# Finishing a masked sum in two column halves, and adding the first half of its last block to the common sums

## The chip, the cores and the metric

The kernel runs on one NeuronCore of one Trainium2 chip. The metric is the device time of one execution in microseconds (us), as the median of several runs. Times inside an execution are read from the profiled run and count from the start of its instruction span. The span is shorter than the device time: 82.7 of 84.4 us in the kernel before. In the profile lines PE is TensorE, DVE is VectorE and ACT is ScalarE.

## The reference

```python
B, S, D = 8, 8192, 512          # x [B,S,D] f32, lengths [B] int64, w [D,D] f32
masked = x * (pos < lengths)     # pos = 0..S-1
cs = np.cumsum(masked, axis=1)
mid = cs[b_idx, lengths // 2]    # one row of 512 for each batch
return mid @ w                   # [8, 512] f32
```

Only row `lengths // 2` of the running sum is used. So the kernel has to add the first rows of each batch up to there, and multiply the eight sums by `w`. For this draw of lengths that is 31.25 MB to read; the arithmetic is small.

## The kernel before

The rows arrive in blocks of 512: 128 partitions with four rows each (the "row groups" 0 to 3). TensorE adds a block to the sums by a matmul whose weights are 8 columns wide, one column for each batch. Row group j uses column tile j of the array, so its sums stand in the PSUM partitions from 32j on. The four groups run side by side: a block leaves eight records in the profile, two for each group, and all eight fit into 1.04 us (74.98 to 76.03) although one lasts 0.59:

```python
def add(j, weights, rows):                 # rows: 128 x 512
    return pe.matmul(s_ps[32*j:32*j+B], lhsT=weights, rhs=rows, start=False, stop=False,
                     skip_group_check=True, tile_position=(0, 32*j))
def add_column(j, weights, row):           # column quarter j of a row group, in tile j
    return pe.matmul(t_ps[32*j:32*j+B, :P], lhsT=weights, rhs=row[:, P*j:P*(j+1)], ...)
def tell():                                # a one-column matmul that raises TensorE's semaphore
    pe.matmul(idle_ps[:1, :1], lhsT=tick[:], rhs=tick[:], ...).then_inc(s_pe, 1)
```

After the loop over the usual blocks comes the tail. The last block of the last batch (tile `last`) arrives in three pieces: row groups 0 and 1, then 2, then 3. It never goes to the common sums `s_ps`. It goes by column quarters straight to `t_ps`, the layout that the transposes read. `s_ps` gets there by a copy to `s_sb` and a "fold", a matmul that adds the four row groups and spreads the columns over the tiles:

```python
# TensorE, tail
tell()
... add_last(0)        # waits for piece 0: 2 row groups x 4 quarters of 128 columns into t_ps
... fold_half(0)       # waits for s_sb copy 0
... add_last(1)
... fold_half(1)       # waits for s_sb copy 1
... add_last(2).then_inc(s_pe, 1)
... product: wait for transpose 0, 16 matmuls, wait for transpose 1, 16 matmuls    # o_ps = sums @ w

# VectorE (DVE), tail
dve.wait_ge(s_pe, PE_ALL)                  # the tell
for h in range(2): copy s_sb half h <- s_ps half h          # 128 x 256 each
dve.wait_ge(s_pe, PE_SUM)                  # all of t_ps
for h in range(2): transpose t_sb half h <- t_ps
dve.wait_ge(s_pe, PE_OUT); copy o_ps out                     # ScalarE copies the other half
```

## Time and profile before

| What | Before |
|---|---|
| device time, median of 3 runs | 84.37 us (84.34 to 84.56) |
| instruction span of the profiled run | 82.7 us |
| last usual block landed, its adds | 74.52; 74.98 to 76.03 us |
| the three pieces of `last` landed | 75.80, 76.48, 77.10 us |
| tell ended; the two copies ended | 76.01; 77.01 us |
| first transpose started | 77.73 us |
| product | 78.12 to 79.22 us |

The table is read from the bottom up. The product waits for the first transpose, and that starts 0.72 us after the second copy's end. In between lie fold and last adds. Everything above "tell ended" is set by the stream of loads. The lines themselves stand in the prediction.

### The profile page before, as it was taken

What the parts mean: (1) busy time and instruction counts of PE and PEld (TensorE: products, weight loads), DVE (VectorE), ACT (ScalarE), POOL (GpSimd) and SP (SyncE); (2) the same over time, 40 slices, a digit from 0 to 9 for tenths busy, and PEclk for the clock granted to TensorE, in tenths of its full rate; (3) what the DMA queues carried; (4) which work ended last, traced back from release to release, by engine and by line L of the source; (5) the groups of instructions that cost most, each with busy time, mean ns of one, the idle gap of its engine ahead of it and who ended that gap; (6) DMA issues with size and microseconds to landing.
All of it is one profiled execution on the core that took longest, in us unless ns stands there. A gap on an engine that the chain in (4) does not pass through costs nothing. (4 is left out here: it accounts for less than half of the span.)

```text
span 82.7 us, 1481 instructions
## 1 busy us (share of the span) xinstructions
PE 59.9 (72%) x377; PEld 15.8 (19%) x377; DVE 14.9 (18%) x78; ACT 7.4 (9%) x8; POOL 1.3 (2%) x14
## 2 busy tenths in 40 slices
PE   2980799999275199999291099994927999797730
PEld 2400020512020012321020024220201141112510
DVE  2858887001001000001000000000000000001420
ACT  2999100000000000000000000000000000000020
POOL 5000000000000000000000000000000000000000
PEclk9999999999999858999999999999996599999999
DMA  2899999999999999999999999999999999899000
GB/s 32 281 440 428 468 414 402 439 401 436 436 452 398 402 444 408 412 396 432 451 425 404 454 438 411 429 396 468 412 420 452 396 452 436 377 408 356 1 0 8
DMA packets 3538, 31.25 MB, mean 378 GB/s; under 512 B 530, under 2 KB 546, under 8 KB 1202
## 3 DMA queue, kind: packets, MB, share of 16 engines
q1 hardware_dynamic: 2610, 27.27, 78.3%
q10 hardware_dynamic: 928, 3.97, 12.6%
HBM read 31.23 MB, written 0.02 MB: 378 GB/s over the span
## 5 line engine op out<-in xcount | busy, mean ns | idle before, releaser
L505 PE MATMUL s_ps<-xt,cur 128*8 128x512 f32 x184 | 25.2, 669 | 14.3 <-PEq L148 14.3
L518 PE MATMUL idle_ps<-idle 128*128 128x512 f32 x36 | 20.2, 681 | 0.0
L505 PEld LDWEIGHTS s_ps<-xt,cur 128*8 128x8 f32 x184 | 4.2, 93 | 32.7 <-issue 32.7
L469 DVE TENSOR_TENSOR cur<-since 128x16 f32 x9 | 1.7, 188 | 46.6 <-DVEq L148 46.6
L518 PEld LDWEIGHTS idle_ps<-idle 128*128 128x128 f32 x36 | 6.6, 208 | 14.1 <-issue 14.1
L505 PE MATMUL s_ps<-rem,cur_rem 128*8 128x512 f32 x64 | 8.4, 592 | 0.0
L322 ACT COPY o_sb<-o_ps 8x128 f32<-8x128 f32 x2 | 0.5, 258 | 70.8 <-PE o_ps L598 70.8
L505 PE MATMUL s_ps<-first,cur_first 128*8 128x512 f32 x16 | 3.8, 1040 | 2.9 <-DVE since L353 2.9
L266 ACT ACTIVATE rem<-rem 128x2048 uint32<-128x2048 uint32 x3 | 5.5, 1892 | 0.0
L529 PE MATMUL s_ps<-zero 1*128 1x512 f32 x2 | 2.1, 1136 | 1.6 <-DVE zero L353 1.6
L505 PEld LDWEIGHTS s_ps<-rem,cur_rem 128*8 128x8 f32 x64 | 1.9, 93 | 5.7 <-issue 5.7
L353 DVE COPY s_sb<-s_ps 128x256 f32<-128x256 f32 x2 | 0.8, 425 | 9.5 <-PE idle_ps L522 9.5
L511 PE MATMUL t_ps<-last,e_last 128*8 128x128 f32 x32 | 1.7, 273 | 0.0
L478 DVE COPY cur_rem<-table 128x32 f32 x5 | 0.9, 181 | 3.0 <-DVEq L148 3.0
L264 ACT ACT_TABLE_LOAD x1 | 1.3, 1283 | 1.5 <-PEq L619 1.5
L505 PEld LDWEIGHTS s_ps<-first,cur_first 128*8 128x8 f32 x16 | 0.3, 90 | 5.9 <-DMA first<-in_x_dram 4.4
L598 PE MATMUL o_ps<-wt,t_sb 128*8 128x128 f32 x32 | 1.1, 273 | 0.4 <-DVE t_sb L353 0.4
L353 DVE TENSOR_TENSOR part_a<-since,step_a 1x42 f32<-1x42 f32 (+1 forms) x2 | 1.1, 555 | 0.1
L598 PEld LDWEIGHTS o_ps<-wt,t_sb 128*8 128x8 f32 x32 | 0.8, 89 | 0.7 <-issue 0.7
L511 PEld LDWEIGHTS t_ps<-last,e_last 128*8 128x8 f32 x32 | 0.8, 88 | 0.3 <-DMA last<-in_x_dram 0.2
L511 PE MATMUL t_ps<-s_sb,fold 128*8 128x128 f32 x8 | 0.8, 274 | 0.1
L532 PEld LDWEIGHTS n_ps<-len_f,ones 1*128 1x128 f32 x2 | 0.7, 332 | 1.0 <-DVE above L353 0.5
(68 smaller groups left out, 13.7 us busy)
## 6 DMA issues: line engine op xcount, KB each, us to landing
xt<-in_x_dram SPq DMA_DIRECT2D x10, 2048.0 KB, 13.4
xt<-in_x_dram SPq DMA_DIRECT2D x3, 1024.0 KB, 11.0
first<-in_x_dram SPq DMA_DIRECT2D x2, 1024.0 KB, 8.0
rem<-in_x_dram ACTq DMA_DIRECT2D x3, 512.0 KB, 8.1
wt<-in_w_dram ACTq DMA_DIRECT2D x1, 1024.0 KB, 4.9
rem<-in_x_dram ACTq DMA_DIRECT2D x3, 256.0 KB, 7.5
last<-in_x_dram SPq DMA_DIRECT2D x1, 512.0 KB, 6.0
last<-in_x_dram SPq DMA_DIRECT2D x2, 256.0 KB, 6.2
```

The costliest lines, as they stand in the source:

```text
L264: act.memzero(lens1[:, 2 * B:])
L266: act.memzero(rem[:, q]).then_inc(s_rfree[q], 1)
L322: copy = act.copy(out=o_sb[1][:, j * P:(j + 1) * P], in_=o_ps[64 + 32 * j:64 + 32 * j + B, :P])
L353: do(*args, **kw).then_inc(s_dve, 1)
L469: dve.tensor_tensor(out=cur[:, k], in0=since[:, :B, here].rearrange("p b h -> p h b"), in1=since[:, 1:, here].rearrange("p b h -> p h b"), ...
L478: dve.tensor_copy(out=cur_rem[:, k], in_=rests[:, ds(dve.snap(of, min_val=1, max_val=RR - 1), 1), k].rearrange("p o w -> p (o w)"),).then_ ...
L505: return pe.matmul(s_ps[32 * j:32 * j + B], lhsT=weights, rhs=rows, start=False, stop=False, skip_group_check=True, tile_position=(0, 32 * j))
L511: return pe.matmul(t_ps[32 * j:32 * j + B, :P], lhsT=weights, rhs=row[:, P * j:P * (j + 1)], start=False, stop=False, skip_group_check=Tru ...
L518: pe.matmul(idle_ps[:], lhsT=idle[:], rhs=idle[:, :1].to_broadcast((P, D)), start=True, stop=True)
L529: pe.matmul(s_ps[:], lhsT=zero[:], rhs=zero[:, :1].to_broadcast((1, D)), start=True, stop=False, skip_group_check=True)
L532: pe.matmul(n_ps[:, :B], lhsT=ones[:], rhs=len_f[:], start=True, stop=True).then_inc(s_pe, 1)
L598: mm = pe.matmul(o_ps[32 * j:32 * j + B, :P], lhsT=t_sb[:, kc, :B], rhs=wt[:, kc, j * P:(j + 1) * P], start=(kc == 0), stop=(kc == KC - 1) ...
```

## The change

Its intent: take fold and last adds out of those 0.72 us. If each column half has its own PSUM tensor (a "bank"), semaphore and transpose, half 0 can be folded under the second copy, and half 1 under the first transpose. The core of the diff:

```diff
+    ENDS = [(slice(0, 2), slice(0, D)), (slice(2, 3), slice(0, D)),
+            (slice(3, 4), slice(0, D // 2)), (slice(3, 4), slice(D // 2, D))]   # 4 pieces, was 3
-    t_ps = ps("t_ps", [P, D])
+    t_ps = [ps(f"t_ps{h}", [P, D]) for h in range(2)]                           # two tensors
-    nc.scalar.dma_start(out=wt[:], in_=w.rearrange("(p kc) d -> p kc d", kc=KC))
+    for h in range(2):                                  # w in two contiguous halves
+        nc.scalar.dma_start(out=wt[:, 2*h:2*h+2],
+                            in_=w[D//2*h:D//2*(h+1)].rearrange("(p k) d -> p k d", k=2))
   # TensorE, front
-        keep_busy()              # one idle matmul
-            keep_busy(b)         # b = 0, 1: one more
   # TensorE, tail
+        if has_last:
+            pe.wait_ge(s_last[0], 16)
+            for g in range(2):
+                add(g, e_last[:], last[:, g])           # "the join": piece 0 into s_ps
         tell()
-        add_last(0); fold_half(0); add_last(1); fold_half(1); add_last(2)
+        wait piece 1: add_columns(h, e_last, last[:, 2]) for h in 0, 1    # 4 x 64 columns each
+        wait piece 2: add_columns(0, e_last, last[:, 3])
+        wait copy 0:  add_columns(0, fold, s_sb)  -> semaphore for transpose 0
+        wait piece 3: add_columns(1, e_last, last[:, 3])
+        wait copy 1:  add_columns(1, fold, s_sb)  -> semaphore for transpose 1
   # DVE, tail
-        dve.wait_ge(s_pe, PE_SUM)
         for h in range(2):
+            dve.wait_ge(s_pe, PE_SUM + h)
             transpose half h                            # after BOTH copies, as before
```

The tail is shortened to its order here; the code has `If_cmp` and full arguments. Cut: one more memset, semaphore counts.

## The prediction

> **What bounds the kernel now.** I read the page's slices first, then the chain that ended last, then the timeline of the last eight microseconds, then the records of the tile that holds the last rows.
>
> The page, for the span and the transfers (40 slices of 2.07 us each):
>
> ```profile
> span 82.7 us, 1481 instructions
> ...
> DMA  2899999999999999999999999999999999899000
> ...
> DMA packets 3538, 31.25 MB, mean 378 GB/s; under 512 B 530, under 2 KB 546, under 8 KB 1202
> ```
>
> From the third slice to the thirty-seventh the 16 DMA engines are full. The kernel streams 31.25 MB, and everything up to about 76.5 us is this stream. The change moves the same bytes, so only what follows the stream can change: the tail of some 6 us. The chain shows which part of it is work:
>
> ```profile
> 74.61 0.37 issue
> 74.98 1.04 PE s_ps L505 x8
> 76.03 0.08 PE idle_ps L522
> ...
> 76.13 0.44 DVE s_sb L353
> ...
> 76.61 1.09 PE t_ps L511 x24
> ...
> 77.73 0.26 DVE t_sb L353
> 77.99 0.14 issue
> 78.12 1.10 PE o_ps L598 x32
> ...
> 79.24 0.29 DVE o_sb L353
> 79.53 0.02 issue
> 79.56 0.28 DVE o_sb L353
> ```
>
> Read it as: last adds into the common sums, copy to memory, fold onto the transposable layout (t_ps), transpose, product, copy out. But a chain names only one releaser of each step, so I asked for the last rows' tile and the timeline of the fold:
>
> ```profile
> L248 SPq DMA_DIRECT2D last<-in_x_dram x3: 333/333/333, 69.8 to 70.9; - x3
> ...
> DMA to landing us min/median/max: 6.0/6.1/6.2
> ```
>
> ```profile
> 75.85 0.17 PE L522 MATMUL idle_ps<-tick 128*1 128x1 bf16 x1
> 75.85 0.62 PE L511 MATMUL t_ps<-last,e_last 128*8 128x128 f32 x16
> 76.61 0.28 PE L511 MATMUL t_ps<-s_sb,fold 128*8 128x128 f32 x2
> 76.64 0.28 PE L511 MATMUL t_ps<-last,e_last 128*8 128x128 f32 x2
> ```
>
> The three pieces of the last block land at 69.82 + 6.0 = 75.8, about 70.35 + 6.1 = 76.5 and 70.9 + 6.2 = 77.1 us; the trace's landing records say 75.80, 76.48 and 77.10. The second s_sb copy ends at 77.01. So two things meet at 77.1: the third landing, and the second copy. After it come 0.63 us of fold and last adds up to the transpose at 77.73. That 0.63 us is what the change attacks.
>
> [...]an f32 128x512 matmul over four column tiles leaves eight records, and all eight fit into 1.04 us (74.98 to 76.03) although each lasts 0.60; four start together, and their second records start 0.43 us later. [...]The trace's packets: 2 KB took 86 ns, 4 KB 162, 8 KB 324 in the mean. That is about 38 ns for each KB and some 10 ns fixed. 1 KB loads are not in this trace. [...]its clock records show two half-clock stretches of 3.41 us, from 28.4 and 62.5 us[...].
>
> **The change part by part.**
>
> *Front.* Two idle matmul instructions go (3.81 and 10.56 us, 2.08 us each[...]). TensorE waits for loads there: the first block lands at 8.27, the second at 10.76, the first pair of usual blocks at 16.84. Without them the second block's adds (1.9 us) start at 10.8 and end at 12.7; the three idle matmuls of the first round then bridge to about 16.3 and the first pair starts at its landing near 16.9 instead of 17.31. That frees a buffer 0.4 us sooner, with two 2 MB transfers still queued: no effect on a full stream. The weights come as 4 KB packets instead of 8 KB: 256 x 162 against 128 x 324 ns, the same within 0.05 us. One more memset on the DVE near 13.6 us (0.2 us) is used by nobody before 14.5. Sum: 0 to +0.05.
>
> *Last rows.* The first piece (two row groups, 512 KB) is as before, and I expect it at 75.80. Now it is added to s_ps: two instructions, one in column tile 0 and one in tile 1, each 128x512. That is four records, but in each tile two follow each other at 0.43 us, so four records take as long as the eight of a full block: 0.86 us. The tiles are busy with the last usual block until 75.85, so the adds occupy 75.85 to 76.71. Only then can the one-column matmul that tells the DVE run: 76.71 + 0.17 = 76.88 against 76.01 before. This is the part that was free before: sixteen 128-column records in t_ps ran from 75.85 to 76.47, under the first copy.
>
> *Copies.* The DVE starts 0.117 us after the tell (76.013 to 76.13). First copy 76.99 to 77.42, second at the old distance of 0.459: 77.45 to 77.88. They have not shrunk: 128x256 each, 0.425 us.
>
> *Fold and transposes.* Half 0 of the fold starts 0.054 us after the first copy, at 77.47; eight records of 64 columns, done near 77.75, under the second copy. So the fold has gone from the path, as meant. But the DVE's program puts both copies before the first transpose, so that starts at 77.88 + about 0.05 = 77.93. Before: 77.73. Loss: 0.20 us. The fold of half 1 runs 77.93 to about 78.23, the second transpose 78.28 to 78.53.
>
> *Product.* It starts 0.147 us after the first transpose's end: 78.18 + 0.15 = 78.33 against 78.12. The third quarter of it would come 0.44 us later, at 78.77, when the second transpose is done. So 32 records run through, to 79.39 against 79.18.
>
> *Column halves by DMA.* By the fit above a 1 KB packet is 10 + 38 = 48 ns (an estimate from the trace's packets). Eight for each engine make 0.38 us for each half, against 0.61 for the whole piece before. Landings near 76.9 and 77.3; they are needed at 77.47 and 77.93. Both hidden.
>
> Sum: the copies end at 77.88 instead of 77.01 (+0.87), and the first transpose follows them by 0.05 instead of 0.72 us (-0.67): +0.20 us, and 0.02 at the front. 84.37 + 0.22 is about 84.6 us.
>
> **The rivals.** *It gains as intended.* If the sums were not later, say because the first piece lands well before the usual block is done, copies would end at 77.0, the first transpose would start at 77.1, the second at about 77.75 after the last landing, and the product would end near 78.6: 0.55 us won, 83.8 us. For it: 0.63 us of work really leaves the path. Against it: the tiles' free time (75.85) and the landing (75.80) coincide, and 0.86 us must then be streamed whichever was first. *It is hidden, and the last landing stays the bound:* if the 1 KB packets were far slower than the fit, the second half would land after 77.9 and the end would be set by it. Twice the estimate, 96 ns, gives 0.77 us for each half and a last landing at 78.0: 84.8 us or so.[...]
>
> **Range and chances.** The stream is the same, and all differences worked out lie between -0.55 and +0.5 us, under 1% of 84.4. The runs before spread by 0.22. I predict 84.6 us, 84.25 to 84.95 in 8 of 10. Over 2% is 1.7 us[...]: faster 0.01, within 2% 0.98, slower 0.01.
>
> **What would show it.** In the changed profile the chain should run: s_ps adds from the usual block, then s_ps adds from the last rows (about 0.86 us), the tell, both s_sb copies one after the other, the transpose, the product; no t_ps matmul between copies and transpose. The tell should end some 1.05 us after the first piece's landing. The first transpose should start within 0.1 us of the second copy's end. I am wrong if the first transpose starts less than 1.9 us after the first piece lands, if it waits for a landing, or if the stream itself ends at another time than 76.6 +- 0.2 us.

+0.87, -0.67 and +0.02 us at the front on 84.37 make about 84.6.

## More of the kernel before

One line that looks like nothing will matter later. It fixes the instruction slot at which TensorE's program starts, here 80:

```python
pe.addr_align(256, offset=80, max_nops=0)
```

## The result

The changed kernel took 84.59 us (84.54 to 84.73, four runs) against 84.36 (84.34 to 84.56, four runs) of the kernel before in the same rounds. The ratio is 1.0024, with a 95% interval of 1.0004 to 1.0044: the same within 2%, and 0.2 us slower. Here and below a ratio is the mean time of one kernel's fast runs over that of the other's of the same rounds, so it is not quite the ratio of the medians. Executions over 1.5% slower than the fastest of the same kernel are left out of the means.

The page of the changed kernel, the same lines as in the prediction:

```profile
span 82.9 us, 1505 instructions
...
DMA packets 3827, 31.26 MB, mean 377 GB/s; under 512 B 562, under 2 KB 834, under 8 KB 1618
```

The stream moved the same bytes at the same rate. There are 289 packets more, among them the 1 KB ones (the column "under 2 KB"). The chain of waits of the changed kernel (start us, us, what):

```profile
74.96 1.78 PE s_ps L513 x11
...
76.81 0.09 PE idle_ps L532
...
76.92 0.43 DVE s_sb L360
...
77.38 0.43 DVE s_sb L360
...
77.91 0.26 DVE t_sb L360
...
78.30 1.10 PE o_ps L600 x32
```

Before, the first of these lines was 1.04 us long and the first copy began at 76.13. Now the adds run 0.74 us longer and the copies begin 0.79 later. In return only 0.105 us lies between the second copy (ends 77.80, from its record) and the transpose. Its timeline says which adds they are and where the fold went:

```profile
75.83 1.03 PE L513 MATMUL s_ps<-last,e_last 128*8 128x512 f32 x4
...
76.69 0.17 PE L532 MATMUL idle_ps<-tick 128*1 128x1 bf16 x1
...
77.40 0.30 PE L521 MATMUL t_ps<-s_sb,fold 128*8 128x64 f32 x8 [0.18 <-DVE s_sb L360]
...
77.86 0.30 PE L521 MATMUL t_ps<-s_sb,fold 128*8 128x64 f32 x8
77.91 0.25 DVE L360 STREAM_TRANSPOSE t_sb<-t_ps 128x64 f32<-128x64 f32 x1
```

Read the third line against the chain: the fold of half 0 runs from 77.40 to 77.70, while the second copy runs to 77.80. The last two lines are the two tensors at work: TensorE writes half 1 (77.86 to 78.16) while the DVE reads half 0 (77.91 to 78.16). Whether one tensor would have done for both was not run. The four pieces landed at 75.79, 76.47, 76.83 and 77.11 us. The first came just as the tiles were free for it (its adds start at 75.83), and no landing held the transposes.

So a gain of about 0.6 us and a loss of nearly 0.8 us stand in one kernel. The experiments take them apart.

### The profile page after: what moved, and what is told of

It reads as the page before. It is cut to its first block, busy times and chain, and to the rows that moved or that the text cites. A ratio compares the mean times of both kernels' runs of the same rounds, so it can differ in the third digit from the quotient of the medians.

```text
span 82.9 us, 1505 instructions
## 1 busy us (share of the span) xinstructions
PE 58.8 (71%) x385; PEld 15.4 (19%) x385; DVE 15.0 (18%) x79; ACT 7.4 (9%) x8; POOL 1.3 (2%) x14
## 5 line engine op out<-in xcount | busy, mean ns | idle before, releaser
L528 PE MATMUL idle_ps<-idle 128*128 128x512 f32 x32 | 16.5, 639 | 0.0
L513 PE MATMUL s_ps<-rem,cur_rem 128*8 128x512 f32 x64 | 10.0, 696 | 0.0
L528 PEld LDWEIGHTS idle_ps<-idle 128*128 128x128 f32 x32 | 5.8, 200 | 12.3 <-issue 12.3
L513 PE MATMUL s_ps<-last,e_last 128*8 128x512 f32 x4 | 1.0, 594 | 0.0
L521 PE MATMUL t_ps<-last,e_last 128*8 128x64 f32 x32 | 1.0, 220 | 0.0
L360 DVE TENSOR_TENSOR since<-item,begin 1x42 f32<-1x42 int32 (+1 forms) x2 | 0.8, 422 | 0.1
```

Source lines behind the costliest of these rows:

```text
L360: do(*args, **kw).then_inc(s_dve, 1)
L513: return pe.matmul(s_ps[32 * j:32 * j + B], lhsT=weights, rhs=rows, start=False, stop=False, skip_group_check=True, tile_position=(0, 32 * j))
L521: mm = pe.matmul(t_ps[h][32 * j:32 * j + B, :P // 2], lhsT=weights, rhs=row[:, at:at + P // 2], start=False, stop=False, skip_group_check= ...
L528: pe.matmul(idle_ps[:], lhsT=idle[:], rhs=idle[:, :1].to_broadcast((P, D)), start=True, stop=True)
```

## The experiments

Twelve kernels ran, each in five rounds against the kernel before.

| Run | What it is | Median us | Before, same rounds | Ratio (95%) |
|---|---|---|---|---|
| E1 | changed, columns without the join | 85.49 | 84.44 | 1.0139 (1.0115 to 1.0163) |
| E2 | before, with the join alone | 85.21 | 84.44 | 1.0088 (1.0075 to 1.0101) |
| E3 | changed, join spread over four tiles | 84.53 | 84.44 | 1.0022 (0.9994 to 1.0050) |
| E4 | before, front alone, w strided | 85.74 | 84.44 | 1.0179 (1.0146 to 1.0213) |
| E5 | changed, TensorE program 60 slots later | 85.96 | 84.54 | 1.0157 (1.0132 to 1.0182) |
| E6 | E1, program 64 slots earlier | 86.65 | 84.54 | 1.0243 (1.0209 to 1.0278) |
| E7 | before, front alone, w as in the change | 84.53 | 84.54 | 1.0022 (0.9989 to 1.0056) |
| E8 | changed, program 64 slots earlier | 87.03 | 84.54 | 1.0281 (1.0257 to 1.0304) |
| E9 | changed, join left out (wrong sums) | 84.30 | 84.53 | 0.9967 (0.9949 to 0.9986) |
| E10 | changed, join in one tile | 85.62 | 84.53 | 1.0137 (1.0113 to 1.0160) |
| E11 | E3 with one idle matmul less | 84.48 | 84.53 | 0.9996 (0.9972 to 1.0019) |
| E12 | E11, second copy on ScalarE | 84.11 | 84.53 | 0.9946 (0.9931 to 0.9962) |

My theory: the join puts 0.86 us before the tell, the column halves take about 0.67 us off behind it, and the front does nothing. The first rival: the column halves gain nothing by themselves, because the last landing bounds the end. The second: the front or the transfers cost the difference.

**E1, columns without the join.** Piece 0 goes to the two column tensors after the tell:

```diff
+        tell()
         with pe.If_cmp(has_last, 1, "IS_GE"):
             pe.wait_ge(s_last[0], 16)
             for g in range(2):
-                add(g, e_last[:], last[:, g])
-        tell()
-        with pe.If_cmp(has_last, 1, "IS_GE"):
+                for h in range(2):
+                    add_columns(h, e_last[:], last[:, g])
```

> The changed kernel, but the last block's first two row groups go into the two column banks instead of the common sums, so that the tell to the vector engine waits for the last usual block alone. Theory (the join delays the tell by 0.86 us, all else of the change gains): tell near 76.0, second copy ends near 77.0, the first transpose then waits for the third piece's landing (76.83) and starts near 77.3 instead of 77.9, the product ends near 78.8: about 84.0 us, 0.4 below the kernel before, 0.6 below the changed one. Rival (small transfers or the front cost the 0.2 us): stays at or above 84.5 us.

Measured: 85.49 us, a miss by 1.5. The tail did not explain it: it only began later, with the last usual adds at 76.22 instead of 74.96.

```profile
76.22 1.03 PE s_ps L513 x6
...
78.58 0.26 DVE t_sb L360
```

From the start of these adds to the first transpose it is 2.36 us, against 2.75 in the kernel before and 2.95 in the changed one. The first piece of `last` landed 1.28 to 1.29 us after the last usual block in all three, so in E1's own trace the tail is 0.39 us shorter than before. Something had delayed the stream itself, although by 74.56 us it had moved 30.5 MB in both kernels. The transfers between 28 and 36 us show it, by queue (packets, MB, share of the 16 DMA engines). E1:

```profile
q1 hardware_dynamic: 217, 2.44, 72.8%
q10 hardware_dynamic: 146, 0.81, 24.9%
q8 instruction: 1, 0.02, 0.8%
```

The changed kernel in the same stretch:

```profile
q1 hardware_dynamic: 238, 2.64, 78.0%
q10 hardware_dynamic: 100, 0.69, 20.7%
```

One packet is new: 16 KB of instructions, at 32.77 us, 1.06 us long, on one of the 16 DMA engines. (The changed kernel has one such packet too, but at 82.27 us, when there is nothing left to delay.) From then on one engine lags. Of a pair of usual blocks near 62 us, 15 of the 16 engines had landed by 62.22 us and the last at 63.50; in the changed kernel these are 62.10 and 62.22.

**E2, the join alone.** The kernel before, one `t_ps`, with the join:

```diff
+        with pe.If_cmp(has_last, 1, "IS_GE"):
+            pe.wait_ge(s_last[0], 16)
+            for g in range(2):
+                add(g, e_last[:], last[:, g])
         tell()
...
-            add_last(0)
```

> The kernel before, with one part of the change alone: the last block's first two row groups are added to the common sums before the tell; transposes, banks and transfers as before. Theory: the tell and both copies move by 0.86 us and nothing is taken off the path behind them: about 85.2 us (84.36 + 0.83). Rival (the join is hidden, as the landing at 77.1 binds): 84.4 us.

Measured: 85.21 us, a hit: +0.74 us by ratio. Its chain of waits has both costs at once, the longer adds and the exposed fold:

```profile
74.90 1.90 PE s_ps L505 x12
...
77.34 1.09 PE t_ps L511 x24
```

So the changed kernel's +0.2 is not the join being cheap. The column halves give back some 0.54 us of it (0.0088 - 0.0024, times 84.4).

**E3, the join spread over four tiles.** Two row groups by two column halves, four matmuls of 256 columns:

```diff
             for g in range(2):
-                add(g, e_last[:], last[:, g])
+                for h in range(2):
+                    j, cols = 2 * g + h, slice(D // 2 * h, D // 2 * (h + 1))
+                    pe.matmul(s_ps[32 * j:32 * j + B, cols], lhsT=e_last[:], rhs=last[:, g, cols], ...)
```

> The changed kernel, but the two row groups that join the common sums are cut into column halves and spread over all four column tiles (four 128x256 matmuls, one in each tile) instead of two 128x512 in two tiles. Same arithmetic. Theory (a tile takes its records one after the other, tiles run side by side): adds take 0.43 instead of 0.86 us, tell and transpose 0.43 earlier: about 84.17 us. Rival (the adds wait for something else, or TensorE is bound by the number of columns): 84.6 us as the changed kernel.

Measured: the tail did as expected, the time did not (84.53 us for 84.17). The chain:

```profile
74.96 1.04 PE s_ps L513 x8
76.00 0.45 PE s_ps L581 x8
...
77.51 0.26 DVE t_sb L360
```

The transpose starts 0.40 us earlier than in the changed kernel. The time is another matter: three runs at 84.24 to 84.32 and three at 84.75 to 84.92, so the median says little. Some of the longer ones have a span no longer than the short ones (82.3 and 82.4), and 0.6 us more outside it. The profiled execution (84.32 us) is a short one, so no trace shows where a long one loses its time.

**E4, the front alone.** The kernel before without the two idle matmuls, with one more memset, and w in two transfers. To keep its layout for the old product I cut each partition's 8 KB of w in two, so the halves read 4 KB pieces at a pitch of 8 KB:

```diff
-    nc.scalar.dma_start(out=wt[:], in_=w.rearrange("(p kc) d -> p kc d", kc=KC))
+    for h in range(2):
+        nc.scalar.dma_start(out=wt[:, 2*h:2*h+2],
+                            in_=w.rearrange("(p kc) d -> p kc d", kc=KC)[:, 2*h:2*h+2])
-        keep_busy()
-            keep_busy(b)
```

> The kernel before with the front of the change alone: no idle matmuls before the first blocks, weights in two transfers of 4 KB packets, one more memset. Theory: no effect, 84.36 to 84.45 us. Rival (the front costs the 0.2 us, through the clock or the transfers): 84.6 us.

Measured: 85.74 us, a miss by 1.3. This cut of w is not the change's. The next kernel has the change's own.

**E7, the same front with w in contiguous halves**, as in the change. The order of w's rows is then not that of the old sums, so the result is wrong (relative error 1.4); the work is the same.

```diff
-                            in_=w.rearrange("(p kc) d -> p kc d", kc=KC)[:, 2*h:2*h+2])
+                            in_=w[D//2*h:D//2*(h+1)].rearrange("(p k) d -> p k d", k=2))
```

> The kernel before with the front of the change, now with each weight transfer reading one contiguous half of w as the changed kernel does (the run before it read 4 KB pieces 8 KB apart). The product is wrong on purpose, as the rest of the kernel expects the other layout. Theory (the slow front of that run came from the strided reads of w, not from the missing idle matmuls): 84.35 to 84.5 us. Rival (the missing idle matmuls or the split as such cost time): 85.7 us.

Measured: 84.53 against 84.54 us, 0.03 above the expected range and far from the rival's 85.7. Four runs took 84.39 to 84.63 us, two 85.04 and 85.19, and the interval leaves room for 0.2 us. The profiled runs speak against a cost of the front: the last usual block landed at 74.50 us in the changed kernel and at 74.52 before. The windows from 2 to 4 us differ in their last two columns, DMA share and GB/s. E4, then E7:

```profile
2.00:4.00 2.00, 1.88 (x4) 0.74 (x3) 1.56 (x9) 1.93 (x3) 0.11 (x1) 1.00 0.88 217
```

```profile
2.00:4.00 2.00, 1.88 (x4) 0.74 (x3) 1.56 (x9) 1.93 (x3) 0.11 (x1) 1.00 0.99 371
```

From 4 to 6 us it is 363 against 395. The rate of this one window scatters: the changed kernel, with the same contiguous reads, had 317, and the kernel before 274, and in both the last usual block landed at 74.5 us. What sets E4 apart is the spread of the 16 engines: by the first block it was 1.7 us (first at 7.21, last at 8.91 us; in E7 7.10 and 7.47), and it was still there at piece 0 of `last` (75.72 to 76.87). Only the addresses that w is read from differ between E4 and E7; why they do this stays open.

**E5, the changed kernel with one number changed.** Counted in the built programs, a f32 matmul takes four instruction slots (in the profile too: the join's two matmuls left four weight loads and four matmuls). With its start at slot 80, TensorE's program ends near slot 497 in the kernel before, 502 in the changed one, and 556 in E1. My new theory: it is the later end that brought E1 its instruction packet in the middle of the stream. Started 60 slots later, the changed kernel ends near 562 and should get one too. The rival: E1's order of work does it.

```diff
-        pe.addr_align(256, offset=80, max_nops=0)
+        pe.addr_align(256, offset=140, max_nops=0)
```

> The changed kernel with one number changed: TensorE's program starts at slot 140 instead of 80[...]. No instruction is added or removed. Counted from the build, its program then ends at slot 562 instead of 502[...]. Theory[...]: an instruction packet of 16 KB near 32.7 us, the last landing of each transfer 1.2 us later than the fifteenth, 85.8 us. Rival (the slowness came from the 64-column adds themselves): 84.6 us as the changed kernel.

Measured: 85.96 us, a hit. The instruction packet between 28 and 36 us is there again:

```profile
q8 instruction: 1, 0.02, 0.8%
```

It is at 32.21 us and took 1.07 us; piece 0 of `last` lands at 77.13 instead of 75.79. Not one instruction of the work has changed. So the fetch costs 1.1 us by ratio (0.0157 - 0.0024, times 84.5), and 1.3 us by span (84.2 against 82.9).

**E6 and E8, the start moved the other way.** This was to free E1 of its fetch (E6, ends near slot 492), with the changed kernel at the same start as a control (E8):

```diff
-        pe.addr_align(256, offset=80, max_nops=0)
+        pe.addr_align(256, offset=16, max_nops=0)
```

> The columns-only kernel again (nothing joins the common sums), with TensorE's program starting at slot 16, so that it ends at slot 492[...]. Theory (the join costs 0.86 us on the path, and the rest of the change gains): no instruction packet in the stream, tell near 76.0, first transpose near 77.3, about 84.0 us. Rival (the columns-only form is slow for its own sake): 85.5 us again.

> Control for the columns-only run at slot 16: the changed kernel with TensorE's program at slot 16 and nothing else changed. Theory:[...] 84.6 us as the changed kernel. Rival[...]: off by more than 0.2 us.

Measured: 86.65 and 87.03 us, both misses. Each now has its instruction packet near the start, at 2.86 us (1.66 us long) in E6 and at 3.19 us (0.96 us long) in E8, and one engine lags by over 2 us to the end. E6 also ran part of its tail at half the clock (0.50 from 76 to 78 us). By the count E8's program ends near slot 438, before the 502 of the changed kernel, so a late end does not explain its fetch; why a start at slot 16 brings one was not shown. E6 is 0.38 us faster than E8, in the direction of my theory, but nothing rests on so disturbed a pair. Columns without the join and without a fetch, and with right results, were not measured cleanly.

**E9, the changed kernel without the join.** The two adds are left out, so the last batch is wrong (relative error 0.135). The program ends earlier than the changed kernel's (near 494), and its profile shows no instruction packet:

```diff
             pe.wait_ge(s_last[0], 16)
-            for g in range(2):
-                add(g, e_last[:], last[:, g])
         tell()
```

> The changed kernel without the two adds of the last block's first two row groups; nothing takes their place, so the last batch's row is wrong on purpose. TensorE's program gets shorter by 8 slots and ends at 494. Theory (the join is the 0.86 us on the path, and the third piece's landing at 76.83 binds next): tell near 76.0, first transpose near 77.3 instead of 77.9, about 84.0 us. Rival (something else of the change holds the end): 84.6 us.

Measured: 84.30 us, ratio 0.9967. That is 0.48 us under the changed kernel by ratio (0.0024 + 0.0033, times 84.5), for 0.6 expected. The tail is as expected, and its chain says what bounds it then:

```profile
68.59 7.79 DMA last<-in_x_dram
...
76.43 0.80 PE t_ps L521 x32
...
77.25 0.26 DVE t_sb L360
```

The transpose starts at 77.25 instead of 77.91. It is now held by the pieces of `last`: the chain goes back to the second piece (76.38), because the adds run on from there without a gap. The third piece landed at 76.73, its adds start at 76.78, and the fold of half 0 follows right behind them. The spans of the six runs (82.1 to 82.6 us) are about 0.4 us shorter than the changed kernel's (82.7 to 82.9). The time outside the span is 1.75 to 2.21 us against 1.82 to 1.85, and takes part of the gain back.

**E10, the join in one tile.** Both row groups in column tile 0, so four records stand in one line instead of two and two:

```diff
-                add(g, e_last[:], last[:, g])
+                add(0, e_last[:], last[:, g])
```

> The changed kernel with both adds in column tile 0 instead of one in tile 0 and one in tile 1: same instructions, same slots, right result. Theory (records of one tile follow each other, tiles run side by side): the adds take 1.71 instead of 0.86 us, and as they are on the path all of that comes through: 85.45 us. Rival (the two adds already ran one after the other, or there is slack behind them): 84.6 us.

Measured: 85.62 us, a hit. The chain's first line is now 2.39 us against 1.78:

```profile
74.83 2.39 PE s_ps L513 x12
```

In E3, E10 and the changed kernel the same adds have been placed in four, one and two tiles. The first transpose starts at 77.51, 78.62 and 77.91 us.

**E11, E3 with fewer slots.** My guess for E3's scatter was that its program, ending near slot 510, is so long that some executions have a fetch and others, like the profiled one, none. One idle matmul less in the loop brings it to 506:

```diff
-        BUSY = [3, 1, 0]
+        BUSY = [2, 1, 0]
```

> The four-tile form of the join again, with one idle matmul less in each round of the loop, so that TensorE's program ends at slot 506 instead of 510. Theory (three of six runs of the four-tile form were 0.6 us over the others[...]): all runs near 84.15 us, none near 84.9. Rival: two groups of runs again, median 84.5 us.

Measured: 84.21 to 84.78 in the fast runs (84.48 in the median), and one slow run of 86.17. A miss: the scatter stays, and so does the time outside the span (1.78 to 2.19 us). My guess falls; the cause of the scatter is open.

**E12, E11 with the second copy on ScalarE.** The prediction's loss is that both copies stand before the first transpose in the DVE's program. ScalarE is idle there:

```diff
+        act.wait_ge(s_dve, DVE_ALL + 1)            # after the first copy
+        act.copy(out=s_sb[:, D // 2:], in_=s_ps[:, D // 2:]).then_inc(s_act, 1)
...
-        for h in range(2):
-            step(dve.tensor_copy, out=s_sb half h, in_=s_ps half h)
+        step(dve.tensor_copy, out=s_sb[:, :D // 2], in_=s_ps[:, :D // 2])
...
-        pe.wait_ge(s_dve, DVE_ALL + 2)
+        pe.wait_ge(s_act, 1)
         add_columns(1, fold[:], s_sb[:]).then_inc(s_pe, 1)
```

> The run before it, with the second copy of the common sums on ScalarE instead of VectorE, so that the first transpose waits for the first half's fold and not for the second copy. Theory (after the four-tile join the two copies one after the other hold the first transpose): first transpose near 77.35 instead of 77.5, product ends near 78.75, about 83.95 us, 0.5 below the kernel before. Rival (the second half becomes the bound, through ScalarE's copy or the last landing): 84.15 us or more.

Measured: 84.11 us (83.99 to 84.16), right results; between the theory's 83.95 and the rival's 84.15. It beats both kernels: 0.46 us under the kernel before by ratio (0.0054 x 84.5), for 0.5 expected. Its timeline:

```profile
75.68 0.62 PE L582 MATMUL s_ps<-last,e_last 128*8 128x256 f32 x8
...
76.37 0.42 DVE L362 COPY s_sb<-s_ps 128x256 f32<-128x256 f32 x1 [11.53 <-PE idle_ps L533]
76.83 0.37 ACT L327 COPY s_sb<-s_ps 128x256 f32<-128x256 f32 x1 [67.88 <-DVE s_sb L362]
...
77.22 0.25 DVE L362 STREAM_TRANSPOSE t_sb<-t_ps 128x64 f32<-128x64 f32 x1 [0.42 <-PE t_ps L522]
...
77.61 1.06 PE L604 MATMUL o_ps<-wt,t_sb 128*8 128x128 f32 x32
```

The transpose starts 0.02 us after ScalarE's copy ends, and in E12 it waits for TensorE's adds (the bracket of the fourth line), no longer for a copy. From the tell's end it comes 0.94 us later, against 1.08 in E11 (76.21 to 77.29), so the moved copy is worth 0.14 us. Between the times of E11 and E12 lie 0.42 us (0.0050 x 84.5); I take the rest for the scatter of E11, but no run shows it. That scatter did not show in E12's six runs, at the same slots.

## Why the prediction was right

The time was 84.59 us for a predicted 84.6, and the steps came out one by one:

| Step of the prediction | Predicted us | Measured us |
|---|---|---|
| piece 0 lands | 75.80 | 75.79 |
| tell ends | 76.88 | 76.86 |
| second copy ends | 77.88 | 77.80 |
| first transpose starts | 77.93 | 77.91 |
| second transpose starts | 78.28 | 78.26 |
| product starts, last record ends | 78.33, 79.39 | 78.30, 79.36 |
| the two column pieces land | 76.9, 77.3 | 76.83, 77.11 |
| one 1 KB packet of the loads | 48 ns | 47.9 ns |

*The join (+0.86).* Right, and shown: left out, the transpose starts 0.66 us earlier (E9), and alone it costs 0.74 us (E2). That the cost is the fill of the tiles and not the number of rows is shown by E3 and E10.

*Copies.* Two small sizes were off and cancelled, which is luck: the first copy began 0.06 us after the tell instead of 0.117, and the transpose 0.105 after the second copy instead of 0.05. That just misses the prediction's own sign, "within 0.1 us".

*Fold off the path (-0.67).* Right. The changed kernel's chain has no fold, and E2, which keeps the old order, shows what it would cost. That the DVE's program holds the first transpose behind the second copy is shown by E12, which takes that copy away: 0.14 us less from the tell to the transpose.

*Front (0 to +0.05).* Right for the change as written (E7, within its interval of -0.1 to +0.6%). But its reason was too thin: by packet sizes alone E4 would have been free as well, and it cost over 1 us. The packets were of the same size; where they were read from was not.

*Rivals.* "It gains as intended" fell with the join. "The last landing stays the bound" fell for the changed kernel (last landing 77.11, needed at 77.8), but in E9, with the join gone, the third of the four pieces holds the first transpose. That fewer idle matmuls slow the clock was shown by no trace. The granted clock was 1.00 up to 18 us in both kernels. After that the changed kernel had three stretches of 3.41 us at a clock of 0.50 (from 24.1, 41.2 and 48.0 us) and the kernel before two (from 28.4 and 62.5 us), and the last usual block landed at 74.50 and 74.52 us. The first pair of usual blocks starts at 16.87 us, for a predicted 16.9, but by luck: it landed at 16.56 instead of 16.84, and its adds waited another 0.31 us.

*What no step saw.* Why the change should join piece 0 to the common sums at all. The prediction only counted the cost. E1, the plain alternative, needs 14 matmul instructions more, ends near slot 556 and is 1.2 us slower than the kernel before by ratio. Its fetch is the same packet (16 KB), at nearly the same point (32.77 and 32.21 us), with a like lag (1.2 and 1.4 us at the last landing) as in E5, where the slots alone were changed. So I take the fetch for E1's cause. That E1 without it would gain is supported by its own tail (0.39 us shorter than before) and by E9; a whole kernel without join and fetch, with right results, was not measured. A limit on the slot where TensorE's program ends, somewhere between 510 and 556, fits the profiles of the runs that start at slot 80 or 140: those ending at 494 to 510 (the kernel before, the changed one, E3, E9 and E12) show no instruction packet before 82 us, those ending near 556 and 562 (E1, E5) show one in the stream. It does not fit E8. Such a limit would also explain the two idle matmuls removed at the front: they pay for the slots of the column halves (93 matmuls in both kernels). Whether that was the intent, the runs cannot say.

The fetch was not hidden: one packet of 16 KB, 1.07 us long on one engine, made the kernel 1.1 us slower by ratio (E5). And the one late engine of 16 held the work: in E5 piece 0 of `last` had landed in full at 77.13 us and its adds start at 77.2, in E1 the last usual adds start at 76.22 us instead of 74.96.

## What to carry to other kernels

Work that is moved ahead of a "done" signal costs its streaming time, and in these runs that followed the fullest column tile: from the first of the adds to the tell it took 0.86 us in two tiles, 0.43 spread over four (E3) and 1.72 in one (E10). In this stream, whose DMA engines are busy for 90% or more of nearly every slice of the page from the third to the thirty-fifth, an engine that an instruction packet had put behind never caught up: at the last landing it was still 1.2 to 2.3 us behind the fifteenth (E1, E5, E6, E8; in E1 1.28 us at 62 us and 1.21 at the end). So count instruction slots and look for instruction packets in the trace before blaming the work. And ask which engine's program order holds the next step: spreading the join brought the first transpose forward by 0.40 us (E3), moving one copy to an idle engine by another 0.14, and with both the kernel gained 0.46 us (E12) where the restructured tail alone had gained nothing.
